# Cross-entropy with label smoothing on one Trainium2 core: the results of two blocks of 128 rows turned into rows by TensorE and stored as 512 contiguous bytes each

## The chip, the cores and the metric

The kernel runs on one core of one Trainium2 chip. The metric is device time in microseconds (us) of one execution; a smaller number is better. A profiled execution also gives a span, from the first to the last instruction, which is 1.8 to 2.2 us less than the time of the same execution in the traces quoted here.

## The reference

```python
batch, num_classes = 256, 32000          # logits f32, labels int, smoothing 0.1
log_probs = logits - np.max(logits, axis=-1, keepdims=True)
log_probs = log_probs - np.log(np.sum(np.exp(log_probs), axis=-1, keepdims=True))
# smooth_targets: smoothing / num_classes everywhere, plus 1 - smoothing at the label
return (-np.sum(smooth_targets * log_probs, axis=-1)).astype(np.float32)
```

For each row three numbers are needed: the sum of exponentials, the sum of the logits, and the logit at the label. The result of a row is log(sum of exp) plus a linear part (`lin`). All 32.77 MB of logits have to be read once.

## The kernel before

Each of the 128 partitions holds two neighbouring rows (2p and 2p+1), which are treated as two passes r = 0 and 1. Tiles of a row's columns are loaded from the queue of SP (SyncE, which here does nothing but issue DMAs) into a ring of three buffers, the small tiles of the second pass into buffers of their own. ScalarE computes exp with its sum, VectorE the plain sum. Each sum is a column: one number on each partition.

```python
WIDTHS = (
    (8000, 8000, 8000, 8000),
    (7872, 6400, 4736, 3584, 2752, 2176, 1728, 1472, 1280),
)
# ... (pools, activation table)
    x = logits.rearrange("(p r) c -> p (r c)", r=R)
    lab = small.tile([P, 2 * R], I32, name="lab", tag="lab")
    nc.scalar.dma_start(
        out=lab[:], in_=labels.bitcast(I32).rearrange("(p f) -> p f", p=P)
    )
# ... (index of the label's logit, gather from GpSimd)
    for r in range(R):
        # ...
        for t, w in enumerate(ws):
            if w >= RING_MIN:
                xt = ring.tile([P, max(WIDTHS[0])], FP32, name="xt", tag="xt")
            else:
                xt = tail.tile([P, w], FP32, name=f"xl{t}", tag=f"xl{t}")
            nc.sync.dma_start(out=xt[:, :w], in_=x[:, col : col + w])
            # ... VectorE: sum of xt -> xsum; ScalarE: exp of xt, sum -> esum
            # ... at t == n - 2: se_pre, lin_pre from all tiles but the last
        # ... lin = -c_small * xsum[last] + lin_pre
        nc.scalar.activation(
            out=lse[:], in_=esum[:, n - 1 : n], func=AF.Ln, bias=se_pre[:]
        )
        nc.vector.tensor_tensor(
            out=res[:, r : r + 1], in0=lse[:], in1=lin[:], op=ALU.add
        )
    nc.sync.dma_start(out=out.rearrange("(p r) -> p r", r=R), in_=res[:])
```

The softmax here doesn't subtract the row's maximum and nothing guards it: scores larger than these inputs give would overflow.

Of the kernel before, what the change touches and what calls it, by code (L numbers as in the profile page):

```python
# [6 lines left out]

FP32 = mybir.dt.float32
BF16 = mybir.dt.bfloat16
I32 = mybir.dt.int32  # L10
ALU = mybir.AluOpType
AF = mybir.ActivationFunctionType
# [10 lines left out]
def _exp_ln_table(arch: str) -> int | None:  # L23
    try:
        tables = hw_specs.get_activation_tables(arch)
    except Exception:
        return None
    for i, (_, funcs) in enumerate(tables.items()):
        if {AF.Exp, AF.Ln, AF.Copy}.issubset(funcs):
            return i  # L30
    return None


@with_exitstack
def kernel(
    ctx: ExitStack,
    tc: tile.TileContext,
    logits: bass.AP,
    labels: bass.AP,
    smoothing: bass.AP,  # L40
    out: bass.AP,
):
    nc = tc.nc
    B, C = logits.shape
    P = nc.NUM_PARTITIONS
    R = B // P
    assert B == R * P and len(WIDTHS) == R
    assert all(sum(ws) == C for ws in WIDTHS)
    eps = float(smoothing)
    c_small = eps / float(C)  # L50
    c_big = 1.0 - eps

    ring = ctx.enter_context(tc.tile_pool(name="ring", bufs=3))
    tail = ctx.enter_context(tc.tile_pool(name="tail", bufs=1))
    junk = ctx.enter_context(tc.tile_pool(name="junk", bufs=1))
    small = ctx.enter_context(tc.tile_pool(name="small", bufs=1))

    tbl = _exp_ln_table(nc.m.arch)
    if tbl is not None:
        nc.scalar.add_instruction(  # L60
            mybir.InstLoadActFuncSet(
                name=nc.get_next_instruction_name(),
                act_func_set_id=tbl,
                ins=[],
                outs=[],
            )
        )


    x = logits.rearrange("(p r) c -> p (r c)", r=R)  # L70

    lab = small.tile([P, 2 * R], I32, name="lab", tag="lab")
    nc.scalar.dma_start(
        out=lab[:], in_=labels.bitcast(I32).rearrange("(p f) -> p f", p=P)
    )
    rowoff = small.tile([P, R], I32, name="rowoff", tag="rowoff")
    for r in range(R):
        nc.gpsimd.iota(  # L78
            out=rowoff[:, r : r + 1],
            pattern=[[0, 1]],  # L80
            base=r * C,
            channel_multiplier=R * C,
        )
    flat_idx = small.tile([P, R], I32, name="flat_idx", tag="flat_idx")
    nc.gpsimd.tensor_tensor(  # L85
        out=flat_idx[:],
        in0=rowoff[:],
        in1=lab[:].rearrange("p (r two) -> p r two", two=2)[:, :, 0:1],
        op=ALU.add,
    )  # L90
    gat = small.tile([P, R], FP32, name="gat", tag="gat")
    for r in range(R):
        nc.gpsimd.indirect_dma_start(  # L93
            out=gat[:, r : r + 1],
            out_offset=None,
            in_=logits[:],
            in_offset=bass.IndirectOffsetOnAxis(ap=flat_idx[:, r : r + 1], axis=1),
        )

    res = small.tile([P, R], FP32, name="res", tag="res")  # L100
    col = 0
    for r in range(R):
        ws = WIDTHS[r]
        n = len(ws)
        esum = small.tile([P, n], FP32, name=f"esum{r}", tag=f"esum{r}")
        xsum = small.tile([P, n], FP32, name=f"xsum{r}", tag=f"xsum{r}")
        se_pre = small.tile([P, 1], FP32, name=f"se_pre{r}", tag=f"se_pre{r}")
        sx_pre = small.tile([P, 1], FP32, name=f"sx_pre{r}", tag=f"sx_pre{r}")
        lin_pre = small.tile([P, 1], FP32, name=f"lin_pre{r}", tag=f"lin_pre{r}")
        lin = small.tile([P, 1], FP32, name=f"lin{r}", tag=f"lin{r}")  # L110
        lse = small.tile([P, 1], FP32, name=f"lse{r}", tag=f"lse{r}")
        for t, w in enumerate(ws):
            if w >= RING_MIN:
                xt = ring.tile([P, max(WIDTHS[0])], FP32, name="xt", tag="xt")
            else:
                xt = tail.tile([P, w], FP32, name=f"xl{t}", tag=f"xl{t}")
            nc.sync.dma_start(out=xt[:, :w], in_=x[:, col : col + w])  # L117
            col += w
            h = w // 2
            jd = junk.tile([P, max(WIDTHS[0]) // 2], FP32, name="jd", tag="jd")  # L120
            nc.vector.scalar_tensor_tensor(  # L121
                out=jd[:, :h],
                in0=xt[:, :h],
                scalar=1.0,
                in1=xt[:, h:w],
                op0=ALU.mult,
                op1=ALU.add,
                accum_out=xsum[:, t : t + 1],
            )
            ja = junk.tile([P, max(WIDTHS[0])], BF16, name="ja", tag="ja")  # L130
            nc.scalar.activation(  # L131
                out=ja[:, :w],
                in_=xt[:, :w],
                func=AF.Exp,
                accum_out=esum[:, t : t + 1],
            )
            if t == n - 2:

                nc.vector.tensor_reduce(  # L139
                    out=sx_pre[:], in_=xsum[:, : n - 1], axis=AX.X, op=ALU.add  # L140
                )
                nc.vector.tensor_scalar(  # L142
                    out=lin_pre[:],
                    in0=sx_pre[:],
                    scalar1=-c_small,
                    scalar2=None,
                    op0=ALU.mult,
                )
                nc.vector.scalar_tensor_tensor(  # L149
                    out=lin_pre[:],  # L150
                    in0=gat[:, r : r + 1],
                    scalar=-c_big,
                    in1=lin_pre[:],
                    op0=ALU.mult,
                    op1=ALU.add,
                )
                nc.vector.tensor_reduce(  # L157
                    out=se_pre[:], in_=esum[:, : n - 1], axis=AX.X, op=ALU.add
                )
        nc.vector.scalar_tensor_tensor(  # L160
            out=lin[:],
            in0=xsum[:, n - 1 : n],
            scalar=-c_small,
            in1=lin_pre[:],
            op0=ALU.mult,
            op1=ALU.add,
        )
        nc.scalar.activation(  # L168
            out=lse[:], in_=esum[:, n - 1 : n], func=AF.Ln, bias=se_pre[:]
        )  # L170
        nc.vector.tensor_tensor(  # L171
            out=res[:, r : r + 1], in0=lse[:], in1=lin[:], op=ALU.add
        )
    nc.sync.dma_start(out=out.rearrange("(p r) -> p r", r=R), in_=res[:])


# [33 lines left out]
```

## Time and profile before

| | before |
|---|---|
| time, median of 4 runs | 87.83 us (87.5 to 87.98) |
| span of the profiled run | 85.7 us |
| DMA, 20 to 40 us | 435 GB/s |
| ScalarE, 60 to 79 us | 18.78 of 19 us busy |
| last accumulator read to the store's issue | 81.31 to 81.85 us |
| store's issue to the end of the span | 81.85 to 85.7 us |

The way to read it is told in the prediction. Two lines more, both from the waits of the SP queue (who waited for what: us in total, times, longest):

```profile
SPq L174 <- DVE res L171: 23.3, 1, 23.3
SPq L205 <- DMA out_dram<-res: 2.3, 1, 2.3
```

The SP queue waits 23.3 us for the result before the one store, which does no harm there because all loads are already out (the last was issued at 50.91 us). After the store it waits another 2.3 us for the landing; that wait is bare, at the very end.

### The profile page before, as it was taken

The page shows a single profiled execution, that of the slowest core. Times are in us where ns is not written, and L with a number is a line of the kernel's source. Part 1 is how long each engine was busy: PE and PEld are TensorE (multiplying, and loading weights), DVE is VectorE, ACT ScalarE, POOL GpSimd, SP SyncE. Part 2 cuts the span into 40 slices and gives each one's busy share as a digit, 9 for nine tenths or more (in the row PEclk, how much of TensorE's full clock was granted, in tenths as well). Part 3 has the DMA queues.
Part 4 walks back from the last instruction along what each step waited for, and adds up shares of the span by engine and source line. Part 5 has one row for each costly group of instructions (what it writes and reads, how often), then busy time and mean ns, then how long its engine had stood idle before and what let it go on. Part 6 is the DMA issues. An engine that isn't in the chain of part 4 may idle for free.

```text
span 85.7 us, 167 instructions
## 1 busy us (share of the span) xinstructions
DVE 37.3 (44%) x38; ACT 59.1 (69%) x29; POOL 6.5 (8%) x9
## 2 busy tenths in 40 slices
DVE  0000009900495009920694029706909294566700
ACT  5000009992499709992599829996999999999900
POOL 1000008973000000000000000000000000000000
DMA  7699899997999989999899989989999999997000
GB/s 209 269 433 433 344 463 478 433 463 343 433 478 433 448 358 433 478 433 460 367 397 470 470 382 418 490 354 424 442 431 428 394 425 424 413 415 323 0 1 0
DMA packets 2224, 32.77 MB, mean 382 GB/s; under 512 B 560, under 2 KB 560, under 8 KB 944
## 3 DMA queue, kind: packets, MB, share of 16 engines
q1 hardware_dynamic: 2016, 32.77, 90.3%
q10 hardware_dynamic: 144, 0.00, 0.1%
q0 software_dynamic: 64, 0.00, 0.1%
HBM read 32.77 MB, written 0.00 MB: 382 GB/s over the span
## 4 chain that ended last, share of the span: by engine, by line
DMA 58%; ACT 34%; issue 2%; SPq 1%; DVE 0%; ACTq 0%
DMA xt<-in_logits_dram 58%; ACT ja L131 33%; SPq L117 1%; ACT lse L168 0%; DVE res L171 0%; ACTq L131 0%
## 5 line engine op out<-in xcount | busy, mean ns | idle before, releaser
L131 ACT ACTIVATE ja<-xt 128x8000 bf16<-128x8000 f32 (+2 forms) x6 | 39.8, 6630 | 21.5 <-DMA xt<-in_logits_dram 21.5
L121 DVE SCALAR_TENSOR_TENSOR jd<-xt 128x4000 f32<-128x4000 f32 (+2 forms) x6 | 25.1, 4175 | 31.0 <-DMA xt<-in_logits_dram 31.0
L131 ACT ACTIVATE ja<-xl 128x4736 bf16<-128x4736 f32 (+6 forms) x7 | 16.2, 2314 | 0.3
L121 DVE SCALAR_TENSOR_TENSOR jd<-xl 128x2368 f32<-128x2368 f32 (+6 forms) x7 | 10.3, 1476 | 7.7 <-DMA xl<-in_logits_dram 7.7
L85 POOL TENSOR_TENSOR flat_idx<-rowoff,lab 128x2 int32<-128x2 int32 x1 | 4.1, 4084 | 12.2 <-DMA lab<-in_labels_dram 12.2
L93 POOL DMA_INDIRECT gat<-in_logits_dram,flat_idx x2 | 2.1, 1028 | 0.6 <-issue 0.3
L171 DVE TENSOR_TENSOR res<-lse,lin 128x1 f32<-128x1 f32 x2 | 0.3, 160 | 3.5 <-ACT lse L168 3.5
L60 ACT ACT_TABLE_LOAD x1 | 1.3, 1283 | 0.7 <-PEq L191 0.7
L131 ACT ACTIVATION_READ_ACCUMULATOR ja<-xl 128x1 f32 x7 | 1.3, 186 | 0.0
L157 DVE TENSOR_REDUCE se_pre<-esum 128x1 f32<-128x3 f32 (+1 forms) x2 | 0.3, 158 | 2.1 <-ACT ja L131 2.1
L131 ACT ACTIVATION_READ_ACCUMULATOR ja<-xt 128x1 f32 x6 | 1.1, 186 | 0.0
L168 ACT ACTIVATE lse<-esum,se_pre 128x1 f32<-128x1 f32 x2 | 0.6, 294 | 0.1
L121 DVE DVE_READ_ACCUMULATOR jd<-xl 128x1 f32 x7 | 0.6, 82 | 0.0
L121 DVE DVE_READ_ACCUMULATOR jd<-xt 128x1 f32 x6 | 0.5, 82 | 0.0
L149 DVE SCALAR_TENSOR_TENSOR lin_pre<-gat,lin_pre 128x1 f32<-128x1 f32 x2 | 0.3, 159 | 0.1
L139 DVE TENSOR_REDUCE sx_pre<-xsum 128x1 f32<-128x3 f32 (+1 forms) x2 | 0.3, 158 | 0.1
L160 DVE SCALAR_TENSOR_TENSOR lin<-xsum,lin_pre 128x1 f32<-128x1 f32 x2 | 0.3, 158 | 0.1
L142 DVE TENSOR_SCALAR lin_pre<-sx_pre 128x1 f32<-128x1 f32 x2 | 0.3, 154 | 0.1
L78 POOL IOTA rowoff<- 128x1 int32 x2 | 0.2, 118 | 0.4 <-PEq L205 0.4
L191 POOL MEMSET const-uint8-127<- 128x1 uint8 x1 | 0.1, 118 | 0.0
L191 POOL MEMSET const-float32-0.0<- 128x1 f32 x1 | 0.1, 98 | 0.2 <-issue 0.2
L191 POOL MEMSET const-bfloat16-1.0<- 128x1 bf16 x1 | 0.1, 113 | 0.0
(1 smaller groups left out, 0.1 us busy)
## 6 DMA issues: line engine op xcount, KB each, us to landing
xt<-in_logits_dram SPq DMA_DIRECT2D x4, 4000.0 KB, 21.5
xt<-in_logits_dram SPq DMA_DIRECT2D x1, 3936.0 KB, 21.3
xt<-in_logits_dram SPq DMA_DIRECT2D x1, 3200.0 KB, 19.4
xl<-in_logits_dram SPq DMA_DIRECT2D x1, 2368.0 KB, 24.6
xl<-in_logits_dram SPq DMA_DIRECT2D x1, 1792.0 KB, 28.4
xl<-in_logits_dram SPq DMA_DIRECT2D x1, 1376.0 KB, 31.3
xl<-in_logits_dram SPq DMA_DIRECT2D x1, 1088.0 KB, 33.4
xl<-in_logits_dram SPq DMA_DIRECT2D x1, 864.0 KB, 35.0
```

The costliest lines, as they stand in the source:

```text
L60: nc.scalar.add_instruction(mybir.InstLoadActFuncSet(name=nc.get_next_instruction_name(), act_func_set_id=tbl, ins=[], outs=[],))
L85: nc.gpsimd.tensor_tensor(out=flat_idx[:], in0=rowoff[:], in1=lab[:].rearrange("p (r two) -> p r two", two=2)[:, :, 0:1], op=ALU.add,)
L93: nc.gpsimd.indirect_dma_start(out=gat[:, r : r + 1], out_offset=None, in_=logits[:], in_offset=bass.IndirectOffsetOnAxis(ap=flat_idx[:, r ...
L117: nc.sync.dma_start(out=xt[:, :w], in_=x[:, col : col + w])
L121: nc.vector.scalar_tensor_tensor(out=jd[:, :h], in0=xt[:, :h], scalar=1.0, in1=xt[:, h:w], op0=ALU.mult, op1=ALU.add, accum_out=xsum[:, t ...
L131: nc.scalar.activation(out=ja[:, :w], in_=xt[:, :w], func=AF.Exp, accum_out=esum[:, t : t + 1],)
L139: nc.vector.tensor_reduce(out=sx_pre[:], in_=xsum[:, : n - 1], axis=AX.X, op=ALU.add)
L142: nc.vector.tensor_scalar(out=lin_pre[:], in0=sx_pre[:], scalar1=-c_small, scalar2=None, op0=ALU.mult,)
L149: nc.vector.scalar_tensor_tensor(out=lin_pre[:], in0=gat[:, r : r + 1], scalar=-c_big, in1=lin_pre[:], op0=ALU.mult, op1=ALU.add,)
L157: nc.vector.tensor_reduce(out=se_pre[:], in_=esum[:, : n - 1], axis=AX.X, op=ALU.add)
L168: nc.scalar.activation(out=lse[:], in_=esum[:, n - 1 : n], func=AF.Ln, bias=se_pre[:])
L191: nc = _bacc.Bacc("TRN2", target_bir_lowering=False, num_devices=1)
```

## The change

The intent is a store in one contiguous piece. A column of 128 results is scattered over 128 partitions, so it goes out in 128 pieces of 8 bytes (the trace of the kernel before has 128 packets of 8 B for it). The change maps the rows in two blocks (row r*128+p on partition p), lets TensorE add the last two parts of the sum of exponentials and turn them into a row of 128 by multiplying with an identity matrix, takes the logarithm on the row, and stores 512 bytes for each block, at the end of the block.

```diff
-    x = logits.rearrange("(p r) c -> p (r c)", r=R)
-    lab = small.tile([P, 2 * R], I32, name="lab", tag="lab")
+    lab = small.tile([P, R, 2], I32, name="lab", tag="lab")
     nc.scalar.dma_start(
-        out=lab[:], in_=labels.bitcast(I32).rearrange("(p f) -> p f", p=P)
+        out=lab[:], in_=labels.bitcast(I32).rearrange("(r p two) -> p r two", r=R, two=2)
     )
 ... (row offsets for the gather in the new mapping; a PSUM pool is added, res and the outer col go)
+    ident = small.tile([P, P], FP32, name="ident", tag="ident")
+    make_identity(nc, ident[:])
     for r in range(R):
+        col = 0
 ...
-            nc.sync.dma_start(out=xt[:, :w], in_=x[:, col : col + w])
+            nc.sync.dma_start(out=xt[:, :w], in_=logits[r * P : (r + 1) * P, col : col + w])
 ...
-        nc.scalar.activation(
-            out=lse[:], in_=esum[:, n - 1 : n], func=AF.Ln, bias=se_pre[:]
-        )
+        se_t = psum.tile([1, P], FP32, name=f"se_t{r}", tag=f"se_t{r}")
+        nc.tensor.matmul(
+            se_t[:], lhsT=se_pre[:], rhs=ident[:], start=True, stop=False
+        )
+        nc.tensor.matmul(
+            se_t[:], lhsT=esum[:, n - 1 : n], rhs=ident[:], start=False, stop=True
+        )
+        lin_t = psum.tile([1, P], FP32, name=f"lin_t{r}", tag=f"lin_t{r}")
+        nc.tensor.transpose(out=lin_t[:], in_=lin[:], identity=ident[:])
+        lse_t = small.tile([1, P], FP32, name=f"lse_t{r}", tag=f"lse_t{r}")
+        nc.scalar.activation(out=lse_t[:], in_=se_t[:], func=AF.Ln)
+        lin_row = small.tile([1, P], FP32, name=f"lin_row{r}", tag=f"lin_row{r}")
+        nc.vector.tensor_copy(out=lin_row[:], in_=lin_t[:])
+        res_t = small.tile([1, P], FP32, name=f"res_t{r}", tag=f"res_t{r}")
         nc.vector.tensor_tensor(
-            out=res[:, r : r + 1], in0=lse[:], in1=lin[:], op=ALU.add
-        )
-    nc.sync.dma_start(out=out.rearrange("(p r) -> p r", r=R), in_=res[:])
+            out=res_t[:], in0=lse_t[:], in1=lin_row[:], op=ALU.add
+        )
+        nc.sync.dma_start(
+            out=out[r * P : (r + 1) * P].rearrange("(g i) -> g i", g=1), in_=res_t[:]
+        )
```

More of the change, by code (lines that the diff above doesn't have):

```diff
@@ L6 @@
 from concourse._compat import with_exitstack
+from concourse.masks import make_identity
 FP32 = mybir.dt.float32
@@ L56 @@
     small = ctx.enter_context(tc.tile_pool(name="small", bufs=1))
+    psum = ctx.enter_context(
+        tc.tile_pool(name="psum", bufs=1, space=bass.MemoryType.PSUM)
+    )
     tbl = _exp_ln_table(nc.m.arch)
@@ L80 @@
             pattern=[[0, 1]],
-            base=r * C,
-            channel_multiplier=R * C,
+            base=r * P * C,
+            channel_multiplier=C,
         )
@@ L87 @@
         in0=rowoff[:],
-        in1=lab[:].rearrange("p (r two) -> p r two", two=2)[:, :, 0:1],
+        in1=lab[:, :, 0:1],
         op=ALU.add,
@@ L98 @@
         )
-    res = small.tile([P, R], FP32, name="res", tag="res")
-    col = 0
+    ident = small.tile([P, P], FP32, name="ident", tag="ident")
+    make_identity(nc, ident[:])
     for r in range(R):
+        col = 0
         ws = WIDTHS[r]
@@ L110 @@
         lin = small.tile([P, 1], FP32, name=f"lin{r}", tag=f"lin{r}")
-        lse = small.tile([P, 1], FP32, name=f"lse{r}", tag=f"lse{r}")
         for t, w in enumerate(ws):
```

## The prediction

Two terms in it, a product on TensorE and an add of 128 elements, were my estimates: the trace of the kernel before shows neither.

> **What bounds the kernel now.** I read the page's strip of 40 slices first, then the chain that ended last, the DMA issues, the waits of the SP queue, and last the timeline at the two places where a block ends. The strip and the shares, with stretches asked one by one:
>
> ```profile
> DMA  7699899997999989999899989989999999997000
> 20.00:40.00 20.00, 9.29 (x8) 13.93 (x4) 0.00 (x0) 1.00 1.02 435
> 60.00:79.00 19.00, 11.32 (x13) 18.78 (x13) 0.00 (x0) 1.00 0.99 416
> by line: DMA xt<-in_logits_dram 58.1%; ACT ja L131 33.3%; issue 1.8%; SPq L117 0.9%; ACT lse L168 0.4%; DVE res L171 0.2%; ACTq L131 0.0%
> ```
>
> The columns of a stretch are DVE, ACT and POOL busy us, clock, DMA share and GB/s. The DMA engines are full from about 2 us to 79 us, at 416 to 435 GB/s; 32.77 MB at 430 GB/s is 76 us of the 85.7 us span. ScalarE (exp) fits under it until about 58 us, after which DMA and exp run side by side (18.78 of 19 us busy), because the last tiles were sized so. So any time in which the DMA queue runs dry before 60 us should come out at the end nearly whole. The queue stays full because loads are issued far ahead:
>
> ```profile
> 39.13 0.33 SPq L117 DMA_DIRECT2D xt<-in_logits_dram  x1
> 39.51 2.45 SPq L117 DMA_DIRECT2D xl<-in_logits_dram  x5
> xt<-in_logits_dram SPq DMA_DIRECT2D x1, 3200.0 KB, 19.4
> ```
>
> The first line is the sixth load (6400 columns, 3200 KB); it is issued as soon as the third tile's exp frees its ring buffer, 19.4 us before it lands. The tail loads follow. At that moment only the rest of the fourth load and the fifth (7872 columns) are still queued. The end of block 0 and the end of the kernel:
>
> ```profile
> 41.63 6.87 ACT L131 ACTIVATE ja<-xt 128x8000 bf16<-128x8000 f32 x1 [2.52 <-DMA xt<-in_logits_dram]
> 48.41 0.19 ACT L131 ACTIVATION_READ_ACCUMULATOR ja<-xt 128x1 f32 x1
> 48.63 0.29 ACT L168 ACTIVATE lse<-esum,se_pre 128x1 f32<-128x1 f32 x1
> 48.95 0.16 DVE L171 TENSOR_TENSOR res<-lse,lin 128x1 f32<-128x1 f32 x1 [2.85 <-ACT lse L168]
> 50.92 6.76 ACT L131 ACTIVATE ja<-xt 128x7872 bf16<-128x7872 f32 x1 [2.00 <-DMA xt<-in_logits_dram]
> 58.58 5.54 ACT L131 ACTIVATE ja<-xt 128x6400 bf16<-128x6400 f32 x1 [0.81 <-DMA xt<-in_logits_dram]
> ...
> 79.94 1.27 ACT L131 ACTIVATE ja<-xl 128x1280 bf16<-128x1280 f32 x1
> 80.88 0.16 DVE L160 SCALAR_TENSOR_TENSOR lin<-xsum,lin_pre 128x1 f32<-128x1 f32 x1
> 81.12 0.19 ACT L131 ACTIVATION_READ_ACCUMULATOR ja<-xl 128x1 f32 x1
> 81.34 0.29 ACT L168 ACTIVATE lse<-esum,se_pre 128x1 f32<-128x1 f32 x1
> 81.66 0.16 DVE L171 TENSOR_TENSOR res<-lse,lin 128x1 f32<-128x1 f32 x1 [0.63 <-ACT lse L168]
> 81.85 0.35 SPq L174 DMA_DIRECT2D out_dram<-res  x1
> ```
>
> In block 0 the result is ready at 49.11 and nothing waits for it; in block 1 everything from 81.31 on is bare: Ln, add, store issue, and the store's landing, which the list of issues puts 2.9 us after 81.85.
>
> [...] the SP queue's own waits have 28.5 us for L117 on VectorE and 23.3 us for the store on VectorE, so whatever stands behind a waiting DMA on SP is not issued. [...] the 2.9 us of the store of now 8-byte pieces is in keeping with a slow write, but no run yet splits it. [...] nothing in this trace shows a product.
>
> **The change, part by part.** The row mapping (blocks of 128 rows instead of pairs) and the label load with 8-byte pieces alter addresses, not bytes: 13 loads of the same widths in the same order, and the labels have until 36.9 us. The identity is built on POOL, which is free then. The operations on TensorE are new, and so is the place of the store.
>
> *Order on SP.* The comparison of the two instruction orders shows the first block's store between the fifth load (7872) and the sixth (6400). It waits for res of block 0. So the sixth load and all seven tail loads, issued from 39.13 us on before, now wait for the end of block 0. This is the term I expect to be largest.
>
> *When block 0's store issues.* Accumulator read ends 48.60. [...] Ln on 1x128: exp takes 6870 ns for 8000 and 1270 ns for 1280 columns, so 0.833 ns an element and 203 ns fixed, 0.31 us; [...] Store issue 0.35 and gaps 0.07: the 6400 load is issued at about 50.43, instead of 39.13.
>
> *What that costs.* The 7872 load lands at 50.92, so its last bytes move near 50.4 (in the last load the DMA share falls to 0.01 in the stretch from 79.25, and it lands at 79.8). A load issued into an empty queue is seen once: the first is issued at 0.74 and lands at 12.96, 12.2 us, while the next lands 9.6 us later. So a cold load takes about 2.6 us more than its streaming time. The 6400 load streams in 58.58 - 50.92 = 7.66 us; cold it lands at 50.43 + 7.66 + 2.6 = 60.7, which is 2.1 late. The start of the kernel may be colder than the middle, so I take **1.9 us**. Its tail loads queue behind it in time, and exp of the tail is back to back with them, so the shift reaches the end.
>
> *The end.* After 81.31 plus shift: [...] Ln 0.31 instead of 0.29; [...] together +1.0. The copy of lin to SBUF runs beside the Ln. The store moves one 512-byte row instead of 128 pieces of 8 B: I take 0.4 off its 2.9 us, a guess between 0 and 1. Net **+0.6**.
>
> Sum: 87.76 + 1.9 + 0.6 = 90.26; I put down 90.2, 2.8% slower.
>
> **Rivals.** (1) *The early store is hidden*: the queue had more than 11 us of work at 39.13, so the late issue might just meet it. For it: 50.43 against last bytes at 50.4 is close. Against it: an issue needs about 1 us to its first bytes (0.74 to between 1.75 and 2.0 us at the start). Then only the end counts: 88.0 to 88.4. (2) *The contiguous store pays*: if 2.9 us falls to under 2, the end breaks even, and the whole is the bubble alone, 89.5. That would fit the change's evident intent; nothing in the trace speaks for its size. (3) *TensorE is slower than I think* [...]: each 0.5 us more counts twice, once in the bubble and once at the end: 91.2. (4) *The row pitch changes the load rate*: rows of one load now lie 128,000 B apart instead of 256,000. [...] 1% would be 0.8 us either way.
>
> **Range and chances.** The bubble may be 1.2 to 2.4, the end 0 to 1.2; both lean on the same product time. That gives 89.1 to 91.2 for 8 in 10. 2% is 89.5; below it needs rival 1, or rivals 2 and a small bubble: 0.22. Faster by 2% would need a second effect that I do not see: 0.02. Slower: 0.76.
>
> **What would show it.** In the changed profile: the SP queue issuing the 6400 load near 50.4 behind the store; a stretch after 50.4 with the DMA share well below 0.9; the wait of exp before the 6400 tile grown from 0.81 to about 2.7 us; the last exp starting near 81.8; from the end of its accumulator read to the start of Ln 0.7 to 0.9 us; [...] the last store landing within 2.0 to 2.9 us. It is wrong if the DMA share has no hole there, if the hole is closed again before the last tile, [...] or if the load rate between 20 and 40 us is not 435 GB/s.

## More of the kernel before

In the list of DMA issues the labels take 12.3 us to land:

```profile
lab<-in_labels_dram ACTq DMA_DIRECT2D x1, 2.0 KB, 12.3
```

## The result

The changed kernel takes 88.82 us (88.7 to 89.11, 4 runs) against 87.83 us. The ratio is 1.0123, with a 95% interval of 1.0085 to 1.0162. A ratio here is the mean time of one kernel's runs over that of the other's in the same rounds, so it is not quite the ratio of the two medians. The kernel became about 1% slower. The prediction was 90.2 us, 2.8% slower, with a range from 89.1 us: the direction was right, but the loss was less than half of what was foretold.

The strip of the changed kernel, DMA busy in tenths in 40 slices of its 87.0 us:

```profile
DMA  8699799999899999999999856997998999999400
```

And three stretches around the end of block 0. In this kernel a stretch has the columns PE, PEld, DVE, ACT and POOL busy us, clock, DMA share and GB/s.

```profile
50.00:51.00 1.00, 0.00 (x0) 0.00 (x0) 0.28 (x1) 0.10 (x1) 0.00 (x0) 1.00 0.01 0
51.00:52.00 1.00, 0.00 (x0) 0.00 (x0) 0.54 (x1) 0.48 (x1) 0.00 (x0) 1.00 1.17 282
52.00:53.00 1.00, 0.00 (x0) 0.00 (x0) 1.00 (x1) 1.00 (x1) 0.00 (x0) 1.00 0.45 128
```

The hole is there: the digits 8, 5 and 6 in the middle of the strip, and 0 GB/s from 50 to 51 us. (A packet counts in the stretch in which it starts, so a share over 1 followed by one below is no contradiction.) The timeline of the same kernel, block 0's end and then the kernel's end (start us, duration us, engine and line, operation, and in brackets the idle time before it and what ended it):

```profile
48.97 0.19 ACT L133 ACTIVATION_READ_ACCUMULATOR ja<-xt 128x1 f32 x1
49.21 0.59 PE L175 MATMUL se_t<-ident,esum 128*1 128x128 f32 x2 [2.12 <-ACT ja L133]
49.83 0.27 ACT L181 ACTIVATE lse_t<-se_t 1x128 f32<-1x128 f32 x1 [0.68 <-PE se_t L175]
50.13 0.28 DVE L185 TENSOR_TENSOR res_t<-lse_t,lin_row 1x128 f32<-1x128 f32 x1 [2.72 <-ACT lse_t L181]
50.44 0.32 SPq L188 DMA_DIRECT2D out_dram<-res_t  x1
50.86 0.35 SPq L119 DMA_DIRECT2D xt<-in_logits_dram  x1
51.52 6.76 ACT L133 ACTIVATE ja<-xt 128x7872 bf16<-128x7872 f32 x1 [1.42 <-DMA xt<-in_logits_dram]
60.94 5.54 ACT L133 ACTIVATE ja<-xt 128x6400 bf16<-128x6400 f32 x1 [2.56 <-DMA xt<-in_logits_dram]
...
83.49 0.19 ACT L133 ACTIVATION_READ_ACCUMULATOR ja<-xl 128x1 f32 x1
83.76 0.58 PE L175 MATMUL se_t<-ident,esum 128*1 128x128 f32 x2
84.38 0.27 ACT L181 ACTIVATE lse_t<-se_t 1x128 f32<-1x128 f32 x1 [0.70 <-PE se_t L175]
...
84.99 0.26 SPq L188 DMA_DIRECT2D out_dram<-res_t  x1
```

and the SP queue's wait for its last store:

```profile
SPq L221 <- DMA out_dram<-res_t: 0.5, 1, 0.5
```

Set against the lines of before, the difference of the two profiled executions splits into five parts:

| where | before | changed | this part |
|---|---|---|---|
| exp of the 7872 tile starts | 50.92 | 51.52 | +0.60 |
| exp of the 6400 tile starts | 58.58 | 60.94 | +1.76 |
| last accumulator read ends | 81.31 | 83.68 | +0.01 |
| last store is issued | 81.85 | 84.99 | +0.77 |
| span ends | 85.7 | 87.0 | -1.8 |

The sum is +1.3 us in the span; the times of these two executions, 89.11 and 87.53 us, differ by 1.6, so some 0.3 us lie outside the span, and no view tells what they are. They come back in other runs: the time exceeds the span by 1.74 to 1.86 us in every execution with a recorded span of the kernel before and of the three experiments below that store columns alone, and by 1.96 to 2.22 us in the executions of all other kernels, but for one of about 1.8 us in each of five of them. So not all of a gain at the end of the span is a gain in time. The medians differ by 1.0 only: the profiled run of the changed kernel was the slowest of its four, that of the kernel before nearly its fastest. The hole behaves as foretold, and the load rate from 20 to 40 us was 432 GB/s against 435, so rival 4 did not come. What nobody foretold is the size of the last row: after its issue the store needed 3.9 us to the end of the span before and 2.0 us now. The wait for its landing went from 2.3 us to 0.5 us.

### The profile page after: what moved, and what is told of

Same layout as the page of the kernel before. It is cut to its first block, busy times and chain, and to the rows that moved or that the text cites. A ratio compares the mean times of both kernels' runs of the same rounds, so it can differ in the third digit from the quotient of the medians.

```text
span 87.0 us, 193 instructions
## 1 busy us (share of the span) xinstructions
PE 3.0 (3%) x10; PEld 0.5 (1%) x10; DVE 38.1 (44%) x40; ACT 59.0 (68%) x29; POOL 7.2 (8%) x11
## 4 chain that ended last, share of the span: by engine, by line
DMA 51%; ACT 41%; DVE 2%; PE 2%; issue 1%; SPq 0%; ACTq 0%
DMA xt<-in_logits_dram 51%; ACT ja L133 40%; PE se_t L175 1%; DVE jd L123 1%; DVE res_t L185 1%; ACT lse_t L181 1%; PE lin_t L179 0%; SPq L188 0%; DVE lin L162 0%; DVE se_pre L159 0%; ACTq L133 0%; SPq L119 0%
## 5 line engine op out<-in xcount | busy, mean ns | idle before, releaser
L172 PE MATMUL se_t<-ident,se_pre 128*1 128x128 f32 x4 | 1.2, 396 | 72.6 <-DVE se_pre L159 72.6
L87 POOL TENSOR_TENSOR flat_idx<-rowoff,lab 128x2 int32<-128x2 int32 x1 | 0.2, 195 | 21.9 <-DMA lab<-in_labels_dram 21.9
L185 DVE TENSOR_TENSOR res_t<-lse_t,lin_row 1x128 f32<-1x128 f32 x2 | 0.6, 280 | 3.3 <-ACT lse_t L181 3.3
L181 ACT ACTIVATE lse_t<-se_t 1x128 f32<-1x128 f32 x2 | 0.5, 267 | 1.4 <-PE se_t L175 1.4
L175 PE MATMUL se_t<-ident,esum 128*1 128x128 f32 x4 | 1.2, 395 | 2.1 <-ACT ja L133 2.1
L179 PE MATMUL lin_t<-ident,lin 128*1 128x128 f32 x2 | 0.7, 372 | 6.6 <-DVE lin L162 6.6
L183 DVE COPY lin_row<-lin_t 1x128 f32<-1x128 f32 x2 | 0.6, 278 | 0.9 <-PE lin_t L179 0.9
```

Of the source, the lines that this page charges most:

```text
L172: nc.tensor.matmul(se_t[:], lhsT=se_pre[:], rhs=ident[:], start=True, stop=False)
L175: nc.tensor.matmul(se_t[:], lhsT=esum[:, n - 1 : n], rhs=ident[:], start=False, stop=True)
L179: nc.tensor.transpose(out=lin_t[:], in_=lin[:], identity=ident[:])
L181: nc.scalar.activation(out=lse_t[:], in_=se_t[:], func=AF.Ln)
L183: nc.vector.tensor_copy(out=lin_row[:], in_=lin_t[:])
L185: nc.vector.tensor_tensor(out=res_t[:], in0=lse_t[:], in1=lin_row[:], op=ALU.add)
```

## The experiments

Four questions: does the hole come from the place of the store on SP (and not from TensorE or from the row layout)? Why does the last store end 1.8 us sooner? What is the +0.6 us ahead of the 7872 tile? And does a version without the hole beat both kernels? Eleven kernels ran, all correct.

### Both stores at the end of the SP queue

```diff
-        nc.sync.dma_start(out=out[r * P : ...], in_=res_t[:])
+        stores.append((r, res_t))
+    for r, res_t in stores:
+        nc.sync.dma_start(out=out[r * P : ...], in_=res_t[:])
```

> The changed kernel with one edit: both row stores are issued at the end of the SP queue, behind all loads. Theory (the hole in the loads comes from the SP queue standing still for block 0's store): the 6400 load is issued near 39.5 us again, no stretch after 50 us with a low DMA share, last accumulator read ends near 81.9 instead of 83.7 us, the end from there unchanged; span about 85.2 us, 1.8 less than the changed kernel, time about 87.1, ratio to before 0.992. Rival (the hole comes from the blocks' row layout or from TensorE's work, wherever the store stands): the 6400 tile's exp still starts near 60.9, time about 88.8, ratio 1.012.

Measured: 87.00 us (86.61 to 87.07), ratio to before 0.9901 (0.986 to 0.9942). Two of the same stretches, in the same columns:

```profile
50.00:51.00 1.00, 0.00 (x0) 0.00 (x0) 0.12 (x1) 0.00 (x0) 0.00 (x0) 1.00 0.96 410
51.00:52.00 1.00, 0.00 (x0) 0.00 (x0) 0.82 (x1) 0.76 (x1) 0.00 (x0) 1.00 1.13 486
```

and the exp of the 6400 tile in the timeline:

```profile
58.84 5.54 ACT L134 ACTIVATE ja<-xt 128x6400 bf16<-128x6400 f32 x1 [0.75 <-DMA xt<-in_logits_dram]
```

No hole, and the idle time before the 6400 tile is 0.75 us instead of 2.56. TensorE's work and the row layout are unchanged here, so the place of the store costs the difference of the two ratios, 2.2% or 1.9 us.

### Both stores from ScalarE's DMA queue, at the same time as in the changed kernel

```diff
-        nc.sync.dma_start(out=out[r * P : ...], in_=res_t[:])
+        nc.scalar.dma_start(out=out[r * P : ...], in_=res_t[:])
```

> The changed kernel with both stores issued from ScalarE's DMA queue instead of SP's; the store of block 0 leaves at the same time as in the changed kernel. Theory (the hole comes from SP standing still in front of the loads, not from the store's own traffic in mid-stream): no hole, 6400 tile's exp near 58.7, ratio like that of the deferred store, 0.990; ScalarE waits for the add of block 0 (1.3 us idle there anyway), so nothing is lost. Rival (the store in mid-stream holds the loads up, as the 4-byte pieces did): the 6400 tile late by 1 us or more, ratio 1.003 or more.

Measured: 86.93 us (86.49 to 87.14), ratio 0.9907 (0.9844 to 0.9971). From its timeline:

```profile
50.17 0.50 ACTq L188 DMA_DIRECT2D out_dram<-res_t  x1
58.86 5.54 ACT L133 ACTIVATE ja<-xt 128x6400 bf16<-128x6400 f32 x1 [0.75 <-DMA xt<-in_logits_dram]
```

The row's store is issued in mid-stream here too, at 50.17 us (by the packet records its packet ran at 53.96, among the loads' packets, and it landed at 55.38), and the 6400 tile is on time. So a 512-byte store among the loads did no harm (6400 tile at 58.86 us, 58.84 with both stores at the end). SP stood still in this kernel too, with one tail load still to issue:

```profile
SPq L119 <- DMA out_dram<-res_t: 3.9, 1, 3.9
```

That cost nothing (ratio 0.9907, against 0.9901 with both stores at the end), because the loads before it were already queued. In the changed kernel the queue of loads ran empty behind SP's wait (0 GB/s from 50 to 51 us), and between the two tiles that cost 1.76 us.

### The kernel before with a store for each pass, the first one ahead of the 6400 load

```diff
+        # inside the loop over r
-    nc.sync.dma_start(out=out.rearrange("(p r) -> p r", r=R), in_=res[:])
+        nc.sync.dma_start(
+            out=out.rearrange("(p r) -> p r", r=R)[:, r : r + 1], in_=res[:, r : r + 1]
+        )
```

> The kernel before with one edit: each block's column of results is stored at the end of its block from the SP queue, so the first store stands between the fifth and the sixth load. No TensorE, old row mapping. Theory: res of block 0 is ready at 49.1, so the 6400 load is issued near 49.6 instead of 39.1, about 0.7 us earlier against the loads than in the changed kernel; the hole costs 1.0 to 1.2 us, exp of the 6400 tile starts near 59.7, time about 88.9, ratio 1.013. The final store still lands about 2.9 us after its issue. Rival (the queue's position costs nothing, TensorE or the layout does): ratio 1.000.

Measured: 92.72 us (91.68 to 92.95), ratio 1.0551 (1.0494 to 1.0608). The position costs time without TensorE and with the old mapping, as the theory has it, but over four times as much as I expected. SP issued the 6400 load at 49.51 us, close to the expected 49.6. What follows (columns DVE, ACT, POOL busy, clock, DMA share, GB/s):

```profile
50.00:51.00 1.00, 0.16 (x1) 0.16 (x1) 0.00 (x0) 1.00 3.84 308
51.00:52.00 1.00, 1.00 (x1) 1.00 (x1) 0.00 (x0) 1.00 0.63 51
...
53.00:54.00 1.00, 1.00 (x1) 1.00 (x1) 0.00 (x0) 1.00 0.00 0
```

The load's first packets start in the first stretch, right behind the store's 128 pieces of 4 B on all 16 DMA engines, and 14 of the 16 take 4.2 to 5.4 us by the trace's packet records (a share of 3.84 in one stretch is their length, counted where they start), where most later ones of the same load take 0.95 us. An empty queue explains only a part of that: in the changed kernel the first packets behind the row took 1.3 to 1.9 us. The store landed 4.2 us after its issue, at 53.25, the load at 63.2 instead of 58.5. So here a store in many small pieces ahead of a load on the same queue held the load up, and for longer than its own writes were outstanding: the slow packets ended between 55.2 and 56.2, two to three us after the store had landed. How it does so is not shown. The 512-byte row went over one engine and had landed (at 51.55) before the first packet of the load behind it (51.84).

### The changed row mapping with the old end: columns, stored by blocks at the end

The edit takes the TensorE part out of the kernel with deferred stores and puts Ln and add on a column back, each block stored as 128 pieces of 4 B:

```diff
-            out=out[r * P : ...].rearrange("(g i) -> g i", g=1), in_=res_t[:]
+            out=out[r * P : ...].rearrange("(p o) -> p o", o=1), in_=res[:]
```

> The row mapping of the changed kernel (two blocks of 128 rows, labels in 256 pieces of 8 B) with the end of the kernel before (Ln and add on a column) and one column store of 128 pieces of 4 B for each block, both at the end of the SP queue. Theory: only the start term of 0.4 to 0.6 us remains (tiles 2 to 5 of the stream landing late), the final store lands 2.6 to 3 us after its issue as before; time about 88.3, ratio 1.006. Rival (the fast final store of the changed kernel comes from storing by blocks, half the bytes at the end, not from the row): landing near 1.1 us and time about 86.5, ratio 0.985.

Measured: 92.44 us (91.95 to 92.57), ratio 1.0522 (1.0478 to 1.0567), against an expected 88.3: a miss. The last store left at 81.94 us, as before (81.85), so all of the loss lies behind it. From the waits of the SP queue:

```profile
SPq L208 <- DMA out_dram<-res: 7.3, 2, 4.6
```

The two stores were waited for for 7.3 us in all, up to 4.6 us for one. The store by blocks is not what made the end fast. Half the bytes in the same number of pieces took 7.9 us from issue to landing, more than twice the 2.9 us of the kernel before. The two stores overlapped: by the packet and semaphore records the first one's packets ended at 79.5 us, behind the loads, and it landed at 85.16, 5.6 us later; the second one's packets ended at 82.98 and it landed at 89.84, 6.9 us later. (The 4.7 us "after" the packets in two of the expectations below is the time from the one landing to the other, so theory A was set up with a wrong figure.) The second store's pieces are 4 B at steps of 4 B. The last store of the experiment above had pieces of 4 B too, at steps of 8 B, and the wait for it was 2.2 us. That pointed to how close the pieces lie, and the next four runs ask for it.

### Rows of 512 B in 16 pieces of 32 B, and a row cut into 504 B and 8 B

Both are edits of the kernel with deferred stores. The first pads the row in SBUF so that it has to be stored in pieces:

```diff
-        res_t = small.tile([1, P], FP32, ...)
+        res_w = small.tile([1, 16, 10], FP32, ...)
+        res_t = res_w[:, :, 0:8]
```

> The kernel with deferred stores, each 512-byte row written in 16 pieces of 32 B over the 16 DMA engines. So far: one piece of 512 B lands 0.35 us after its packet, 128 pieces of 8 B (1 KB) 1.9 us after, 128 pieces of 4 B (512 B) 4.7 us. Theory A (pieces that write into the same 64 bytes wait for each other, about 0.25 to 0.29 us each: 8 pieces 1.9, 16 pieces 4.7): 2 pieces to 64 bytes, landing 0.6 us after the packets, 1.4 us from issue to landing, time about 87.3. Theory B (any piece under 512 B is slow by itself): about 1.9 us after the packets or more, time about 88.5. Theory C (all pieces of one 512-byte line wait for each other): 16 pieces, over 4 us, time about 91. Theory D (the count of pieces matters, not their place: 0.015 to 0.035 us each): 0.6 to 0.9 us.

Measured: 87.42 us (87.0 to 87.59, 4 runs), ratio 0.9956 (0.9877 to 1.0035). The last store in the list of DMA issues, with the us from issue to landing at the end of the line:

```profile
out_dram<-res_w SPq DMA_DIRECT2D x1, 0.5 KB, 1.6
```

The trace's packet records put the last packet's end at 84.27 and the landing at 84.60, so 0.33 us after the packets. That is as fast as one piece of 512 B (0.33 us in the changed kernel). It refutes B and C, it lies below the 0.6 to 0.9 us of D, and it also refutes my A in its literal form: two pieces of 32 B in the same 64 bytes did not wait for each other. The 0.5 us by which it lands later after its issue than the unsplit row (1.6 against 1.1) lies before the packets' end: the issue alone took 0.51 us instead of 0.26.

```diff
-        nc.sync.dma_start(out=out[r * P : (r + 1) * P]..., in_=res_t[:])
+        for a, b in ((0, 126), (126, 128)):
+            nc.sync.dma_start(out=out[r * P + a : r * P + b]..., in_=res_t[:, a:b])
```

> The kernel with deferred stores, each row stored as 504 B and, in a DMA of its own behind it, 8 B. Theory A (only pieces in the same 64 bytes at the same time wait for each other): the 8-byte piece shares its 64 bytes with the end of the 504-byte one, so two writes at most: the last landing within 0.7 us of the last packet; the end is about 0.4 us later than with one store, mostly for the second issue. Theory B (a piece of 8 B is slow by itself): the last landing 1.9 us after its packet.

Measured: 87.64 us, one run. The 504-byte piece landed 0.34 us after its packet, the 8-byte piece 0.31 us after its own. A piece of 8 B alone was not slow.

### 128 pieces of 8 B, 64 B apart and side by side, into a scratch tensor

Both are edits of the kernel with one row store (below), which write an extra column to HBM. They differ in one number:

```diff
 ... (pair[:, r] is filled with a copy of lin by VectorE)
+    scratch = nc.dram_tensor("scratch", [P, 16], FP32).ap()   # the other run: [P, 2]
+    nc.sync.dma_start(out=scratch[:, 0:2], in_=pair[:])
```

> The kernel with pair mapping, rows and one 1 KB store, plus a second store of a column of 128 pieces of 8 B into a scratch tensor in HBM, the pieces 64 B apart; it is issued near 81.1 us, before the row. It has the piece size, the piece count and the 16 engines of the store of the kernel before, but no two pieces share 64 bytes. Theory A (small pieces wait for each other only where they fall close together: 8 B and 4 B pieces at 8-byte steps landed 1.9 us after their packets, 4-byte pieces at 4-byte steps 4.7): landing about 0.35 us after the last packet, 1.2 to 1.4 us from issue. Theory D (128 small pieces are slow wherever they go): about 1.9 us after the packets, 2.9 from issue.

> The same with the pieces of the scratch store next to each other, 8 B apart, as the store of the kernel before has them; the control for the spaced one. Theories A and D both expect 1.9 us from the last packet to the landing, 2.9 us from issue; anything near 0.35 would say that the out tensor, not the pattern, was slow.

Measured in one execution each (86.88 and 87.42 us), issue to landing in the last column; first 64 B apart:

```profile
scratch<-pair SPq DMA_DIRECT2D x1, 1.0 KB, 1.6
```

and side by side:

```profile
scratch<-pair SPq DMA_DIRECT2D x1, 1.0 KB, 3.0
```

In both runs the pieces' packets ran from 82.1 to 82.3 us; the landing came 0.55 us after them with room between the pieces and 1.97 us after them without. Same piece size, count, engines and bytes; only the distance differs. So it is shown, with one execution on each side, that these 128 pieces of 8 B landed 1.4 us later because they lay side by side; the late landing itself came in three traces (1.89 us after the packets in the kernel before, 1.97 in the run with 8-byte labels, 1.97 here). How this comes about is not shown: 32-byte pieces side by side were free of it (0.33 us), 8-byte ones were not (1.97), and 4-byte ones side by side were worst (5.6 and 6.9). The 32-byte pieces were only 16, so whether their size or their number freed them was not tested.

### Old mapping, rows by TensorE, one store of 1 KB

```diff
+        # the TensorE end of the changed kernel, res_t = [1, P, R]
+            out=res_t[:, :, r], in0=lse_t[:], in1=lin_row[:], op=ALU.add
+    nc.sync.dma_start(
+        out=out.rearrange("(g i) -> g i", g=1), in_=res_t[:].rearrange("g p r -> g (p r)")
+    )
```

> The row mapping, label load and load addresses of the kernel before, with the TensorE end of the changed kernel for both blocks and one contiguous store of 1 KB at the very end. Theory: no hole, no start term; the end has +0.8 us for TensorE, Ln and add on rows and -1.8 us for the store in one piece: time about 86.8, ratio 0.988, landing about 1.1 us after issue. Rival (the store is fast only because of its 512 B or its block, or the start term is none): landing well over 1.1 us, ratio 0.995 or more; or no difference to the kernel with the deferred stores.

Measured: 86.70 us (86.59 to 86.82), ratio 0.9879 (0.9841 to 0.9918), as expected. The wait for the store:

```profile
SPq L223 <- DMA out_dram<-res_t: 0.5, 1, 0.5
```

This is the lowest time found, though the kernels with deferred stores, with ScalarE's queue and with VectorE's transpose (0.9901 to 0.9907) lie within its noise. It is faster than the kernel before by 1.2%, clear of noise, and by the two ratios to before it is 2.4% faster than the changed kernel.

### VectorE's transpose instead of TensorE

The column is turned into four rows of 32 by one transpose on VectorE, stored in 4 pieces of 128 B, both stores at the end of the queue.

```diff
-        nc.vector.tensor_tensor(out=res[:], in0=lse[:], in1=lin[:], op=ALU.add)
+        nc.vector.tensor_tensor(out=wide[r][:, 0:1], in0=lse[:], in1=lin[:], op=ALU.add)
+        nc.vector.transpose(out=res[:], in_=wide[r][:])      # both [P, 32]
```

> Blocks of 128 rows, end of the kernel before (Ln and add on a column), then VectorE's transpose of 32x32 squares turns the column into 4 rows of 32, stored in 4 pieces of 128 B, both stores at the end of the SP queue. No TensorE. Theory A (pieces in different 64 bytes do not wait for each other): landing about 0.4 us after the packets, 1.1 to 1.2 from issue; from the last accumulator read to the store's issue 0.65 + 0.25 us instead of 1.33 with TensorE, so about 0.4 us faster than the deferred version: time about 86.5, ratio 0.985. Theory B (any piece under 512 B is slow): landing 1.9 us after the packets, time about 88.

Measured: 86.77 us (86.31 to 87.31), ratio 0.9905 (0.9828 to 0.9982). From the timeline:

```profile
81.97 0.21 DVE L180 STREAM_TRANSPOSE res<-wide 128x32 f32<-128x32 f32 x1
82.21 0.51 SPq L183 DMA_DIRECT2D out_dram<-res  x1
```

and from the SP queue's waits:

```profile
SPq L217 <- DMA out_dram<-res: 0.7, 1, 0.7
```

From the end of the last accumulator read (81.36) to the store's issue are 0.85 us, where the version above needs 1.32. But the store in four pieces gives it back: issue 0.51 us instead of 0.32, and 1.55 us from issue to landing instead of the 1.1 to 1.2 that I expected. No gain over the row by TensorE, none lost.

### The labels in 256 pieces of 8 B, in the kernel before

```diff
-    lab = small.tile([P, 2 * R], I32, name="lab", tag="lab")
+    lab = small.tile([P, R, 4], I32, name="lab", tag="lab")
-        out=lab[:], in_=labels.bitcast(I32).rearrange("(p f) -> p f", p=P)
+        out=lab[:, :, 0:2],
+        in_=labels.bitcast(I32).rearrange("(p r two) -> p r two", p=P, two=2),
```

> The kernel before with one edit: the labels are loaded in 256 pieces of 8 B instead of 128 of 16 B, nothing else. In the traces so far the second tile lands at 22.40 to 22.50 us where labels come in 128 pieces (5 traces) and at 22.65 to 23.15 where they come in 256 (7 traces, all with blocks of 128 rows); exp of the 7872 tile starts at 50.84 to 50.99 against 50.97 to 51.52. Theory (the label pieces take turns with the first tiles' packets): labels land near 22.5 instead of 13.1 us, the second tile at 22.6 to 23.1, exp of the 7872 tile at 51.0 to 51.4. Rival (the row pitch of the blocks does it): the second tile at 22.4 to 22.5, exp of the 7872 tile at 50.85 to 51.0.

Measured: 88.02 us against 87.70, one run each, too few. In the list of DMA issues:

```profile
lab<-in_labels_dram ACTq DMA_DIRECT2D x1, 2.0 KB, 23.2
```

and in the timeline:

```profile
51.31 6.76 ACT L132 ACTIVATE ja<-xt 128x7872 bf16<-128x7872 f32 x1 [1.98 <-DMA xt<-in_logits_dram]
```

The labels need 23.2 us to land instead of 12.3, the second tile landed at 22.83, and the 7872 tile's exp starts 0.39 us later than in the profile of before. Without the blocks the delay is there, in this one execution, and beyond all five traces with whole labels, so the label pieces look enough to cause it. How large it is varies, and whether the row pitch adds to it is not separated: the seven traces with blocks lie between 50.97 and 51.52, the five with pairs and whole labels between 50.84 and 50.99.

## Why the prediction was wrong

**The order on SP and the time of block 0's store: right.** The 6400 load was foretold at 50.43 us and issued at 50.86. The accumulator read of block 0 ended 0.56 us later than before (49.16 instead of 48.60), because the tiles ran late already; from there to the load are 1.70 us, foretold 1.83.

**The cost of the hole: right.** Foretold 1.9 us; 1.76 between the two tiles in the trace, 1.9 by undoing the place alone. It reached the end whole: the last accumulator read is 2.37 us late, the 6400 tile 2.36. The cut from the computed 2.1 us to 1.9 was a guess that came out well: from issue to landing the load took 9.99 us (50.86 to 60.85), 2.3 us more than its streaming time of 7.66, where the prediction computed 2.6. From the end of its issue (51.21) to its first packet (51.84) 0.63 us passed, and the first packet of each engine then took 1.3 to 1.9 us, where later ones took 0.95 (at the start of the kernel before 1.5 to 2.3 us, and later 1.19, for packets of 32,000 B).

**The chain at the end: nearly right.** Foretold +1.0 for product, Ln and add; +0.77 measured, mainly because product and handoffs took 0.70 us (83.68 to 84.38), less than my estimate. In the records of the changed kernel a product of 1x128 with the 128x128 identity in fp32 took 0.58 to 0.59 us, the transpose of a column 0.37 us, the add of 128 elements 0.28 us.

**The store: the step that failed.** The prediction said "I take 0.4 off its 2.9 us, a guess between 0 and 1". The store took 1.8 us off the end, outside the guess. Rival 2 had the right term but thought of it as falling to just under 2 us, which merely pays for the chain, and so came to 89.5 (the bubble alone on its 87.76 is 89.7, a slip of the sum); by the semaphore records the store landed 1.1 us after its issue. The mechanism, a cheaper store in one piece, was right; its size was a guess, and the prediction said itself that no run had split the 2.9 us. In fact 1.9 of them passed after the last packet had ended, where the row needed 0.33, and the runs with scratch stores show that 1.4 of those came from the pieces lying side by side. (The remaining 0.3 of the 1.8 us is a shorter way from the issue to the end of the packets: 0.76 us instead of 1.04.)

**The labels: a smaller miss.** "Alter addresses, not bytes" overlooked that the number of pieces doubles (256 packets of 8 B in the trace of the changed kernel, 128 of 16 B in that of before). In the kernel before it cost about 0.4 us, in one execution; in the seven traces with blocks the 7872 tile started 0.05 to 0.6 us later than in the profile of before, so the 0.6 of the changed kernel's profile is explained only in part.

With the measured terms the sum is +0.4 for the labels, +1.8 for the hole, +0.8 for the chain and -1.8 for the store, so +1.2 us in the span, with some 0.3 outside it on top; the timed runs gave +1.0. The terms are read from single executions and close no better than that. The intent of the change was sound, and worth about 1 us net at the end. A store placed between two loads gave it all back and 1 us more.

## What to carry to other kernels

The SP queue issued one DMA after the other, and the store that waited for its result held back the load behind it from 39.13 to 50.86 us. So a store that waits must not stand in front of loads that could go: put it behind them, or on another engine's queue (ratios to before 0.9901 and 0.9907 here, 1.0123 in front of them), and look at the order of the DMA instructions in the trace after every change that moves a store into a loop. It need not be the order of the source: in the runs with a scratch store that store stands last in the source and was issued first (81.28 against 82.65 us). If results lie one to a partition, look at the landing of the last store: here 128 pieces of 8 B side by side landed 1.4 us later than the same pieces spread out, and one contiguous row, 1.8 us sooner at the end, paid for a TensorE product and a longer add, 0.77 us. Count pieces, not bytes, on the side of small loads too: the same 2 KB of labels took 23.2 us to land in 256 pieces and 12.3 us in 128.
